# A two-layer decoder trunk on one core: weight halves formed by GpSimd transfers in the attention stages

## The chip, the cores and the metric

The kernel runs on one core of a Trainium2 chip. The time is device microseconds of one execution. A core has five engines that this text names: TensorE (PE, with its weight loads PEld), VectorE (DVE), ScalarE (ACT), GpSimd (POOL) and SyncE (SP). Each takes its own instructions strictly in order; they meet through semaphores. Transfers between HBM and the on-chip memory (SBUF) are issued by an engine's queue and carried out by 16 DMA engines.

## The reference

Two layers over 512 tokens of width 1024. Each has three parallel attention branches (differential, latent, and cross attention into 256 memory tokens), mixed by gates, and a squared-ReLU MLP of width 4096. All is float32.

```python
for l in range(DEPTH):
    h = rmsnorm(x, g_mix[l])
    dq, dk, dv, c_q, c_kv_kr, xq, gate_logits = jnp.split(h @ w_in[l], split_idx, axis=-1)
    y_diff = diff_attention(dq, dk, dv, ...) @ w_diff_o[l]
    y_mla = latent_attention(c_q, c_kv_kr, ...) @ w_mla_o[l]
    y_mem = memory_cross_attention(xq, rmsnorm(mem, mem_gain[l]), w_mem_kv[l], ...) @ w_cross_o[l]
    gates = jax.nn.sigmoid((gate_logits + b_gate[l]).reshape(B, S, N_BRANCHES, D))
    merged = gates[:, :, 0] * y_diff + gates[:, :, 1] * y_mla + gates[:, :, 2] * y_mem
    x = x + merged @ w_out[l]
    u = rmsnorm(x, g_mlp[l]) @ w_mlp1[l]
    x = x + jnp.square(jax.nn.relu(u)) @ w_mlp2[l]
```

## The kernel before, in words

**Three products for one.** Matmuls with weights run in the type float32r, which keeps fewer bits than float32. To keep the accuracy, each operand is split in two: a high half, which is the value rounded to float32r, and a low half, which is what the rounding lost. `mm3` (L108) multiplies high by high, high by low and low by high into one accumulator, at lines L109, L110 and L111.

**Weights come in units.** A unit is a tile of 128 x 1024 values (512 KB), the weights of one 128-wide output block or of half a 256-wide one; a few are smaller. There are 160 a layer. For each unit, `load_raw` issues a load from SyncE's queue into one of three tiles `wraw`; `do_split` calls `split_into`, in which ScalarE copies the tile into `whi` with rounding (L101) and VectorE subtracts, `wlo = wraw - whi` (L102). There are four buffers of `whi` and four of `wlo`. The loop at the end of the trunk keeps four units split ahead of the one that is used next, and three more loaded.

**The program is a list of entries.** An entry is a piece of a projection (with the units it uses) or a piece of attention (with none). In the attention stages `merge` interleaves the two kinds after the table `PLAN`, so that TensorE has projection matmuls while an attention step goes through softmax. Seven such stages follow each other in a layer: two of latent attention (beside the gates, then the memory's keys and values `w_mem`, the cross queries `w_xq` and the first differential projection `w_d`), one of cross attention and four of differential attention. Before them come the latent projections, after them the last gates, the output projections and the MLP, all without attention. A scheduler then places all instructions on their engines by its own estimate of times; the list gives it the dependencies and the buffers, and it may move instructions past each other.

**An attention step.** TensorE writes scores (`pss`, L610 and L613), VectorE adds the mask and finds the negative row maximum `nmx` (L622, L624), ScalarE takes the exponential into a tile `P` (L627; three buffers of 128 x 2 x 512), TensorE transposes `P` (L638, L654), ScalarE copies, TensorE multiplies by the values. A differential projection (`diff_chunk`, L553) is drained twice per chunk, once for each half of the tokens: ScalarE copies and squares (L564, L566), VectorE sums (L568), GpSimd takes an inverse square root `f` (L132), VectorE rotates meanwhile (L583 to L585) and multiplies by `f` (L587), TensorE transposes (L591). GpSimd does little else.

Of the kernel before, what the change touches and what calls it, by code (L numbers as in the profile page):

```python
# [9 lines left out]
F32 = mybir.dt.float32  # L10
F32R = mybir.dt.float32r
AF = mybir.ActivationFunctionType
ALU = mybir.AluOpType
AX = mybir.AxisListType

P = 128
# [22 lines left out]

class Entry:  # L40
    def __init__(self, fn, units=()):
        self.fn, self.units = fn, list(units)


def merge(att, gemm):
    if not att:
        return gemm
    out, n, m = [], len(att), len(gemm)
    j = 0
    for i, a in enumerate(att):  # L50
        out.append(a)
        while j < m and j * n < (i + 1) * m:
            out.append(gemm[j])
            j += 1
    out.extend(gemm[j:])
    return out
# [3 lines left out]
def tile_trunk(ctx: ExitStack, tc: tile.TileContext, x_t, mem_t, mem_n, pos, ifr, gcol, grow, w_ck, w_cq, w_kvb, w_qb,  # L60
               w_mem, w_xq, w_d, w_g, w_oc, w_om, w_od, w_out, w_1, w_2, out):
    nc = tc.nc
    V, A, G, T = nc.vector, nc.scalar, nc.gpsimd, nc.tensor

    def pool(name, bufs, **kw):
        return ctx.enter_context(tc.tile_pool(name=name, bufs=bufs, **kw))

    RB, NB = 3, 4
    cst = pool("cst", 1)
    sm = pool("sm", 2)  # L70
    pw_raw, pw_hi, pw_lo = pool("wraw", RB), pool("whi", NB), pool("wlo", NB)
    pools = {n: pool(n, b) for n, b in (("H", 16), ("O", 16), ("X", 8), ("G", 1), ("B", 24), ("scr", 5), ("PT", 4))}
    p_p = pool("P", 3)
    PS = {n: pool("ps_" + n, b, space=bass.MemoryType.PSUM) for n, b in (("acc", 2), ("s", 3), ("tp", 2), ("o", 1))}
# [3 lines left out]
    def nm(s):  # L78
        cnt[0] += 1
        return f"{s}{cnt[0]}"  # L80

    def tl(which, dt=F32):
        return pools[which].tile([P, 512], dt, tag=which, name=nm(which))
# [16 lines left out]
    def split_into(hi, lo, src):  # L100
        A.activation(out=hi, in_=src, func=AF.Copy)  # L101
        V.tensor_tensor(out=lo, in0=src, in1=hi, op=ALU.subtract)  # L102
# [116 lines left out]
    def feed(l, k, xt, gbase, dst, sqs):  # L219
        hi, lo = tl(dst, F32R), tl(dst, F32R)  # L220
        split_scaled(hi, lo, xt, gc[:, l, gbase + k:gbase + k + 1])
        if k == 0:
            A.activation(out=sqs, in_=xt, func=AF.Square)
        else:
            s = tl("scr")
            A.activation(out=s, in_=xt, func=AF.Square)
            V.tensor_tensor(out=sqs, in0=sqs, in1=s, op=ALU.add)
        return hi, lo

    def new_sqs():  # L230
        return tl("scr")
# [22 lines left out]
    prog = []  # L254
# [24 lines left out]
    def layer(l):  # L279
# [13 lines left out]
        def begin():  # L293
            if l == 0:
                sqs = new_sqs()
                h = []
                xts = []
                for k in range(KT):
                    xt = tl("X")
                    nc.sync.dma_start(out=xt, in_=x_t[k * P:(k + 1) * P, :])  # L300
                    xts.append(xt)
                    if k in (0, 2, 5):
                        load_raw()
                for k, xt in enumerate(xts):
                    h.append(feed(0, k, xt, C_MIX, "H", sqs))
                st["h"], st["sqs"] = h, sqs
            s["h"] = st["h"]
# [550 lines left out]
        def dpair(p):  # L858
            return diff_chunk(p, 0) + diff_chunk(p, 1) + diff_chunk(p, 2)

        e = [Entry(lambda w: begin())]
        gx = [gate_item(1, ft, "X") for ft in range(KT)]
        ym = [y4_item(w_om, "om", 1, fp, True) for fp in range(4)]
# [10 lines left out]
        def take(spec):  # L874
            r = []
            for t in spec.split():
                n, _, k = t.partition(":")
                k = int(k) if k else len(groups[n])
                r += groups[n][:k]
                groups[n] = groups[n][k:]  # L880
            return r
        phases = [[], mla_att(0) + mla_att(1), mla_att(2) + mla_att(3), cross, diff_att(0) + diff_att(1), diff_att(2) + diff_att(3),
                  diff_att(4) + diff_att(5), diff_att(6) + diff_att(7), []]
        for a, sp in zip(phases, PLAN):
            e += merge(a, take(sp))
        assert not any(groups.values())
        e += [y8_item(ft) for ft in range(KT)]
        e += [out_item(ft) for ft in range(KT)]
# [5 lines left out]
    for l in range(L):  # L894
        prog.extend(layer(l))

    units = [ap for e in prog for ap in e.units]
    raws, splits = [], []
    consumed = 0

    def load_raw():
        ap = units[len(raws)]
        a, b = ap.shape[1], ap.shape[2]
        t = pw_raw.tile([P, 1024], F32, tag="wraw", name=nm("wraw"))
        nc.sync.dma_start(out=t[:, :a * b].rearrange("p (a b) -> p a b", a=a), in_=ap)
        raws.append((t, a, b))

    def do_split():
        t, a, b = raws[len(splits)]
        hi = pw_hi.tile([P, 1024], F32R, tag="whi", name=nm("whi"))  # L910
        lo = pw_lo.tile([P, 1024], F32R, tag="wlo", name=nm("wlo"))
        split_into(hi[:, :a * b], lo[:, :a * b], t[:, :a * b])
        splits.append(tuple(z[:, :a * b].rearrange("p (a b) -> p a b", a=a) for z in (hi, lo)))

    for i, e in enumerate(prog):
        if i == 0:
            e.fn([])
            continue
        while len(splits) < min(len(units), consumed + NB):
            while len(raws) < min(len(units), len(splits) + RB):  # L920
                load_raw()
            do_split()
        while len(raws) < min(len(units), len(splits) + RB):
            load_raw()
        n = len(e.units)
        e.fn(splits[consumed:consumed + n])
        consumed += n


# [79 lines left out]
```

## Time and profile before

| | |
|---|---|
| median of 3 runs | 2035.33 us (2035.23 to 2035.63) |
| the profiled execution | 2039.67 us, of which the span of the profile is 2037.6 |
| layer 0: start and latent projections | 0 to about 130 us |
| layer 0: attention stages | about 130 to 600 us |
| layer 0: output projections and MLP | about 600 to 1020 us |
| layer 1: attention stages | about 1140 to 1607 us |
| bytes read from HBM | 175.06 MB, 88 GB/s over the span |

Busy time on TensorE is an engine's share with matmuls overlapping each other, so a TensorE that is always busy in a stretch did not wait in it. A row of waits names who waited, on which line, and who ended the wait. A granted clock under 1.00 means that TensorE ran slower for part of a stretch.

### The profile page before, as it was taken

Reading aid. Unit: us, or ns where it says so; the run is one execution under the profiler, and the core shown is the slowest. Engines: PE = TensorE matmul, PEld = TensorE weight load, DVE = VectorE, ACT = ScalarE, POOL = GpSimd, SP = SyncE. Lnnn points to the kernel's source line nnn. Section 1 sums busy time; section 2 is a strip of 40 time slices with the busy share of each in tenths; the row PEclk is TensorE's granted clock in tenths of the full one; section 3 lists DMA queues with packets and bytes.
Section 4 is the critical chain, followed back from the end, with each engine's and each line's share of the span. In section 5 each row is a group of like instructions: output and inputs, shape, how many; then the busy total and the mean of one; then the engine's idle time right before and its main releaser. Section 6 shows DMA issues by size and latency. Waiting matters only on the chain.

```text
span 2037.6 us, 27922 instructions
## 1 busy us (share of the span) xinstructions
PE 2005.1 (98%) x11008; PEld 1715.9 (84%) x11008; DVE 1162.2 (57%) x2170; ACT 917.4 (45%) x1727; POOL 146.0 (7%) x121
## 2 busy tenths in 40 slices
PE   8999999999999999999999999999999999999999
PEld 7779997888878888888888899979897788888887
DVE  7755765777656543434447567757686454434442
ACT  6666654444433432323346666634445334323321
POOL 0300110111200000000002001101020000000000
PEclk9989999999999999999999999999999999999999
DMA  5233122222214333333332321222222333333332
GB/s 170 73 110 102 69 63 73 63 73 73 63 53 154 93 96 101 93 99 98 117 104 67 125 80 63 72 74 63 73 63 63 101 116 93 102 96 94 102 94 73
DMA packets 54675, 181.06 MB, mean 89 GB/s; under 512 B 6416, under 2 KB 7440, under 8 KB 54544
## 3 DMA queue, kind: packets, MB, share of 16 engines
q1 hardware_dynamic: 51840, 175.66, 27.8%
q10 hardware_dynamic: 2704, 3.62, 0.6%
q8 instruction: 87, 1.43, 0.3%
q14 instruction: 44, 0.36, 0.1%
HBM read 175.06 MB, written 4.19 MB: 88 GB/s over the span
## 4 chain that ended last, share of the span: by engine, by line
PE 95%; ACT 2%; DVE 1%; DMA 1%; issue 0%; POOL 0%; ACTq 0%; DVEq 0%; POOLq 0%
PE psacc L109 21%; PE psacc L111 20%; PE psacc L110 20%; PE pss L109 7%; PE pss L111 7%; PE pss L110 7%; PE pss L610 2%; PE pss L613 2%; PE pso L642 2%; PE pstp L654 1%; PE pstp L638 1%; PE pstp L591 1%; PE pso L110 1%; PE pso L111 1%; PE pso L109 1%; PE pstp L479 1%
## 5 line engine op out<-in xcount | busy, mean ns | idle before, releaser
L101 ACT ACTIVATE whi<-wraw 128x1024 fp32r<-128x1024 f32 (+3 forms) x320 | 334.5, 1046 | 751.7 <-PE psacc L110 398.5
L102 DVE TENSOR_TENSOR wlo<-wraw,whi 128x1024 fp32r<-128x1024 f32 (+3 forms) x320 | 385.9, 1206 | 97.7 <-ACT whi L101 95.4
L109 PE MATMUL psacc<-H,whi 128*128 128x512 f32 x816 | 321.6, 394 | 2.6 <-ACT B L561 2.2
L110 PE MATMUL psacc<-H,whi 128*128 128x512 f32 x816 | 320.2, 392 | 0.0
L111 PE MATMUL psacc<-H,wlo 128*128 128x512 f32 x816 | 320.1, 392 | 0.0
L109 PE MATMUL psacc<-whi,H 128*128 128x256 f32 (+1 forms) x928 | 271.6, 294 | 10.3 <-ACT whi L101 6.8
L110 PE MATMUL psacc<-wlo,H 128*128 128x256 f32 (+1 forms) x928 | 265.1, 286 | 0.0
L111 PE MATMUL psacc<-whi,H 128*128 128x256 f32 (+1 forms) x928 | 264.3, 287 | 0.2 <-DVE H L106 0.2
L109 PE MATMUL pss<-O,whi 128*128 128x512 f32 x640 | 249.8, 392 | 1.6 <-ACT O L105 1.6
L110 PE MATMUL pss<-O,whi 128*128 128x512 f32 x640 | 250.8, 392 | 0.0
L111 PE MATMUL pss<-O,wlo 128*128 128x512 f32 x640 | 250.5, 392 | 0.0
L109 PEld LDWEIGHTS psacc<-whi,H 128*128 128x128 f32 x928 | 177.6, 192 | 17.8 <-ACT whi L101 6.8
L109 PEld LDWEIGHTS psacc<-H,whi 128*128 128x128 f32 x816 | 153.2, 188 | 36.0 <-ACT B L561 2.6
L111 PEld LDWEIGHTS psacc<-H,wlo 128*128 128x128 f32 x816 | 153.2, 188 | 33.6 <-issue 2.0
L110 PEld LDWEIGHTS psacc<-H,whi 128*128 128x128 f32 x816 | 153.3, 188 | 31.4 <-issue 0.7
L110 PEld LDWEIGHTS psacc<-wlo,H 128*128 128x128 f32 x928 | 178.2, 192 | 1.8 <-issue 1.0
L111 PEld LDWEIGHTS psacc<-whi,H 128*128 128x128 f32 x928 | 177.3, 192 | 1.0 <-DVE H L106 0.4
L840 DVE TENSOR_TENSOR X<-psacc,X 128x512 f32<-128x512 f32 x64 | 44.3, 692 | 207.1 <-PE psacc L111 207.1
L627 ACT ACTIVATE P<-pss,nmx 128x128 f32<-128x128 f32 (+2 forms) x224 | 115.1, 521 | 73.6 <-DVE nmx L624 47.5
L109 PEld LDWEIGHTS pss<-O,whi 128*128 128x128 f32 x640 | 120.4, 188 | 27.3 <-ACT O L105 2.0
L110 PEld LDWEIGHTS pss<-O,whi 128*128 128x128 f32 x640 | 121.1, 189 | 25.5 <-DVE O L106 0.3
L111 PEld LDWEIGHTS pss<-O,wlo 128*128 128x128 f32 x640 | 121.0, 189 | 24.9
(231 smaller groups left out, 3220.6 us busy)
## 6 DMA issues: line engine op xcount, KB each, us to landing
wraw<-in_w_dram SPq DMA_DIRECT2D x128, 512.0 KB, 3.6
wraw<-in_w_g_dram SPq DMA_DIRECT2D x48, 512.0 KB, 3.6
wraw<-in_w_d_dram SPq DMA_DIRECT2D x48, 512.0 KB, 3.6
wraw<-in_w_mem_dram SPq DMA_DIRECT2D x16, 512.0 KB, 3.7
wraw<-in_w_od_dram SPq DMA_DIRECT2D x16, 512.0 KB, 3.6
wraw<-in_w_out_dram SPq DMA_DIRECT2D x16, 512.0 KB, 3.7
X<-in_x_t_dram SPq DMA_DIRECT2D x16, 256.0 KB, 5.4
wraw<-in_w_xq_dram SPq DMA_DIRECT2D x8, 512.0 KB, 4.3
```

Source lines behind the costliest of these rows:

```text
L101: A.activation(out=hi, in_=src, func=AF.Copy)
L102: V.tensor_tensor(out=lo, in0=src, in1=hi, op=ALU.subtract)
L109: T.matmul(o, lhsT=l[0], rhs=r[0], start=first, stop=False, **kw)
L110: T.matmul(o, lhsT=l[0], rhs=r[1], start=False, stop=False, **kw)
L111: T.matmul(o, lhsT=l[1], rhs=r[0], start=False, stop=last, **kw)
L479: T.transpose(tp_[:96, t * P:(t + 1) * P], in_=src[t][:, h * 96:(h + 1) * 96], identity=ident)
L591: T.transpose(tp_[:, h * 256 + t * P:h * 256 + (t + 1) * P], in_=y[:, t * 256 + h * P:t * 256 + (h + 1) * P], identity=ident)
L610: T.matmul(sw[m][:, :max(N, 256)], lhsT=qk[m][0][a], rhs=qk[m][1][b], start=i == 0, stop=i == 2)
L613: T.matmul(sv[m], lhsT=qk[m][0], rhs=qk[m][1], start=True, stop=True)
L627: A.activation(out=pt[:, m, :N], in_=sv[m], func=AF.Exp, bias=nmx[:, m:m + 1], accum_out=ssum[m])
L642: T.matmul(o, lhsT=w[:, j * P:(j + 1) * P], rhs=vs(j), start=j == 0, stop=j == nb - 1)
L840: V.tensor_tensor(out=xt, in0=q, in1=xt, op=ALU.add)
```

## The change

In the attention stages a unit no longer passes through a raw tile. A transfer issued from GpSimd's queue reads the weights from HBM and casts them to float32r straight into `whi`. ScalarE writes the negated high half into `wlo`. A second transfer from GpSimd reads the same weights again and adds them onto `wlo`, which leaves weight minus high half. VectorE has no part in it. An entry is marked `dma` if it stands in a stage with attention: 61 units a layer.

Elsewhere a unit is loaded from SyncE's queue and split as before, except that its raw tile is one of the three buffers `P` of the attention weights; the pool `wraw` is gone. There are six buffers of `whi` (`NBH`) and four of `wlo` (`NBL`). `ahead` begins a load up to six units ahead, makes low halves up to four ahead and two loads behind (`LAG`), and issues the adding transfer one low half behind. The space for the descriptors of GpSimd's transfers is doubled.

```diff
@@ class Entry
-        self.fn, self.units = fn, list(units)
+        self.fn, self.units, self.dma = fn, list(units), False
@@ tile_trunk
-    RB, NB = 3, 4
+    NBH, NBL, LAG = 6, 4, 2
-    pw_raw, pw_hi, pw_lo = pool("wraw", RB), pool("whi", NB), pool("wlo", NB)
+    pw_hi, pw_lo = pool("whi", NBH), pool("wlo", NBL)
@@ layer
         for a, sp in zip(phases, PLAN):
-            e += merge(a, take(sp))
+            g = take(sp)
+            for x in g:
+                x.dma = bool(a)
+            e += merge(a, g)
@@ end of tile_trunk
+    def begin_load():
+        ap, dma = units[len(hi_t)]
         a, b = ap.shape[1], ap.shape[2]
+        if dma:
+            hi = halves(pw_hi, "whi", a, b)
+            G.dma_start(out=hi, in_=ap)
+            hi_t.append(hi)
+        else:
+            t = p_p.tile([P, 2, 512], F32, tag="P", name=nm("wraw")).rearrange("p a b -> p (a b)")[:, :a * b].rearrange("p (a b) -> p a b", a=a)
+            nc.sync.dma_start(out=t, in_=ap)
+            raw_t.append(len(hi_t))
+            hi_t.append(t)
+
+    def make_low():
+        n = len(lo_t)
+        ap, dma = units[n]
+        a, b = ap.shape[1], ap.shape[2]
+        if dma:
+            lo = halves(pw_lo, "wlo", a, b)
+            A.activation(out=lo, in_=hi_t[n], func=AF.Copy, scale=-1.0)
+        else:
+            t = hi_t[n]
+            hi_t[n], lo = halves(pw_hi, "whi", a, b), halves(pw_lo, "wlo", a, b)
+            split_into(hi_t[n], lo, t)
+            raw_t.remove(n)
+        lo_t.append(lo)
+
+    def add_low():
+        nonlocal added
+        ap, dma = units[added]
+        if dma:
+            G.dma_start(out=lo_t[added], in_=ap, accum_op=ALU.add)
+        added += 1
+
+    def ahead(need):
+        while True:
+            n = len(hi_t)
+            if n < len(units) and (n < consumed + NBH if units[n][1] else len(raw_t) < 3 and n < consumed + NBH + 2):
+                begin_load()
+                continue
+            m = len(lo_t)
+            if m < n and m < consumed + NBL and (m < need or m + LAG < n or not units[m][1]):
+                make_low()
+                continue
+            if added < m and (added < need or added + 1 < m):
+                add_low()
+                continue
+            return
@@ kernel
-    nc = _bacc.Bacc("TRN2", target_bir_lowering=False, num_devices=1, dynamic_dma_scratch_size=2048)
+    nc = _bacc.Bacc("TRN2", target_bir_lowering=False, num_devices=1, dynamic_dma_scratch_size=4096)
```

What moves on the engines is seen best at two places of layer 0. The first is GpSimd's queue where the first differential projections are drained. In the rows, `f` is the inverse square root that VectorE multiplies by, `e` and `ss` what it is taken of; the engines in square brackets are those it waits for. Before:

```order
L132 TENSOR_TENSOR f576_2569<-e575_2567,mhalf_120 128x8 [waits DVE_49,Pool_49]
L132 TENSOR_TENSOR f582_2618<-e581_2616,mhalf_120 128x8 [waits DVE_49,Pool_49]
L132 TENSOR_TENSOR f614_2776<-e613_2774,mhalf_120 128x8 [waits DVE_49,Pool_49]
L132 TENSOR_TENSOR f620_2825<-e619_2823,mhalf_120 128x8 [waits DVE_49,Pool_49]
L132 TENSOR_TENSOR f682_3170<-e681_3168,mhalf_120 128x8 [waits DVE_49,Pool_49]
```

At the same place in the changed kernel, where `DMASW` is a transfer from GpSimd's own queue:

```order
L912 DMA whi539_2487<-in_w_d_dram 128x1024 [waits DMASW2_49,PE_49]
L938 DMA wlo540_2489<-in_w_d_dram 128x1024 [waits DMASW3_49,Activation_49]
L132 TENSOR_TENSOR f554_2542<-e553_2540,mhalf_117 128x8 [waits DVE_49,Pool_49]
L912 DMA whi562_2608<-in_w_d_dram 128x1024 [waits DMASW4_49,PE_49]
L938 DMA wlo563_2610<-in_w_d_dram 128x1024 [waits DMASW5_49,Activation_49]
L132 TENSOR_TENSOR f560_2591<-e559_2589,mhalf_117 128x8 [waits DVE_49,Pool_49]
L912 DMA whi566_2663<-in_w_d_dram 128x1024 [waits DMASW6_49,PE_49]
L938 DMA wlo567_2665<-in_w_d_dram 128x1024 [waits DMASW7_49,Activation_49]
L132 TENSOR_TENSOR f590_2747<-e589_2745,mhalf_117 128x8 [waits DVE_49,Pool_49]
```

The inverse square roots followed each other; now a casting load, which waits for TensorE to leave a buffer, and an adding one, which waits for ScalarE, stand between the two `f` of a chunk.

The second place is ScalarE's queue in the memory projections (`w_mem`) of layer 0, where it empties accumulators (`scr<-psacc`, L342). Before:

```order
L101 ACTIVATE O318_1375<-pso367_1540 64x256 [waits DVE_49]
L342 ACTIVATE scr389_1660<-psacc380_1591 128x512 [waits PE_49]
L101 ACTIVATE whi396_1678<-wraw324_1413 128x1024
L344 ACTIVATE scr390_1662<-scr389_1660 128x512 [waits Activation_49]
L101 ACTIVATE whi400_1709<-wraw329_1447 128x1024 [waits DMAHW3_49,PE_49]
L342 ACTIVATE scr417_1782<-psacc399_1684 128x512 [waits PE_49]
L101 ACTIVATE whi424_1800<-wraw383_1620 128x1024 [waits DMAHW0_49]
```

In the changed kernel:

```order
L101 ACTIVATE O311_1363<-pso358_1526 64x256 [waits DVE_49]
L926 ACTIVATE wlo387_1665<-whi319_1430 128x1024 [waits DMASW5_49,DMASW0_49,PE_49]
L342 ACTIVATE scr379_1645<-psacc371_1577 128x512 [waits PE_49]
L926 ACTIVATE wlo390_1695<-whi372_1602 128x1024 [waits DMASW7_49,DMASW2_49,PE_49]
L344 ACTIVATE scr380_1647<-scr379_1645 128x512 [waits Activation_49]
L926 ACTIVATE wlo413_1785<-whi386_1663 128x1024 [waits DMASW4_49,DMASW1_49,PE_49]
L342 ACTIVATE scr405_1765<-psacc388_1668 128x512 [waits PE_49]
```

A rounding copy of a raw tile has become a negated copy of a high half; it waits for a transfer from GpSimd's queue in place of one from SyncE's, and for TensorE to leave a buffer of `wlo`.

More of the change, by code (lines that the diff above doesn't have):

```diff
@@ L302, in begin @@
                     if k in (0, 2, 5):
-                        load_raw()
+                        begin_load()
                 for k, xt in enumerate(xts):
@@ L895, in tile_trunk @@
         prog.extend(layer(l))
[L897 to L902, printed above, removed]
-        a, b = ap.shape[1], ap.shape[2]
[L904 to L913, printed above, removed]
+    units = [(ap, e.dma) for e in prog for ap in e.units]
@@ new lines, in tile_trunk, with halves @@
+    hi_t, raw_t, lo_t = [], [], []
+    added = consumed = 0
+    def halves(pw, tag, a, b):
+        return pw.tile([P, 1024], F32R, tag=tag, name=nm(tag))[:, :a * b].rearrange("p (a b) -> p a b", a=a)
+    def begin_load():
+        ap, dma = units[len(hi_t)]
+        a, b = ap.shape[1], ap.shape[2]
+        if dma:
[7 more added lines that the diff above has]
+            hi_t.append(t)
@@ new lines, in ahead @@
+    def ahead(need):
+        while True:
+            n = len(hi_t)
+            if n < len(units) and (n < consumed + NBH if units[n][1] else len(raw_t) < 3 and n < consumed + NBH + 2):
+                begin_load()
+                continue
[7 more added lines that the diff above has]
+            return
@@ L918, in tile_trunk @@
             continue
[L919 to L924, printed above, removed]
         n = len(e.units)
-        e.fn(splits[consumed:consumed + n])
+        ahead(consumed + n)
+        assert added >= consumed + n
+        e.fn([(hi_t[k], lo_t[k]) for k in range(consumed, consumed + n)])
         consumed += n
```

## The prediction

> **What bounds the kernel now.** I read the page first, then one table of stretches, then the waits of TensorE, then single instructions.
>
> ```profile
> span 2037.6 us, 27922 instructions
> ...
> PE 2005.1 (98%) x11008; PEld 1715.9 (84%) x11008; DVE 1162.2 (57%) x2170; ACT 917.4 (45%) x1727; POOL 146.0 (7%) x121
> ...
> PE 95%; ACT 2%; DVE 1%; DMA 1%; issue 0%; POOL 0%; ACTq 0%; DVEq 0%; POOLq 0%
> ```
>
> The second line gives busy time by engine, the third the chain of waits that ended last. TensorE (PE) is busy for 98% of the span and holds 95% of the chain. The change leaves every matmul in place, so it can win only what TensorE loses by waiting, and only in the attention stages. The table of stretches (columns: stretch in us, its length, busy us of PE, PEld, DVE, ACT and POOL, granted clock, share of the DMA engines, GB/s) shows the two attention parts, each cut at the end of the memory projections, with a piece of the MLP between them:
>
> ```profile
> 130.00:182.00 52.00, 47.43 (x310) 42.23 (x310) 34.82 (x70) 37.46 (x86) 2.71 (x3) 0.90 0.37 119
> 182.00:600.00 418.00, 415.02 (x2718) 365.88 (x2716) 274.80 (x602) 212.32 (x472) 50.74 (x36) 1.00 0.21 66
> 650.00:1000.00 350.00, 350.00 (x1553) 289.92 (x1552) 153.25 (x178) 114.52 (x146) 1.01 (x1) 1.00 0.32 97
> 1140.00:1192.00 52.00, 50.52 (x356) 45.87 (x355) 33.99 (x66) 38.46 (x86) 2.87 (x2) 0.97 0.32 104
> 1192.00:1607.00 415.00, 412.17 (x2680) 362.71 (x2678) 274.70 (x605) 210.51 (x468) 45.12 (x28) 1.00 0.22 67
> ```
>
> TensorE's idle time in the four attention stretches is 4.57 + 2.98 + 1.48 + 2.83 = 11.9 us. The clock takes 0.10 x 52 = 5.2 us and 0.03 x 52 = 1.6 us more. That is the **ceiling** of any gain, some 19 us or 0.9%, although VectorE (DVE) is busy two thirds of these stretches.
>
> How much of it is VectorE's? TensorE's waits (us in total, times, longest) over the whole span, and the four instructions behind one of them (start, length, engine, line, what; in brackets the idle time and who ended it):
>
> ```profile
> PE psacc L109 <- ACT scr L564: 2.2, 2, 1.1
> PE psacc L109 <- ACT B L561: 2.2, 2, 1.1
> ...
> PE pss L610 <- ACT P L627: 0.3, 2, 0.2
> ...
> 502.84 1.22 DVE L102 TENSOR_TENSOR wlo<-wraw,whi 128x1024 fp32r<-128x1024 f32 x1
> ...
> 505.26 0.58 ACT L627 ACTIVATE P<-pss,nmx 128x384 f32<-128x384 f32 x1 [1.07 <-DVE nmx L624]
> ...
> 507.41 0.60 ACT L564 ACTIVATE scr<-psacc 128x512 f32<-128x512 f32 x1
> ...
> 508.06 0.38 PE L109 MATMUL psacc<-whi,H 128*128 128x256 f32 x1 [1.11 <-ACT scr L564]
> ```
>
> VectorE forms a weight's low half for 1.22 us at 502.84; the row maximum behind it comes late, ScalarE (ACT) waits 1.07 us for that, empties the accumulator late, and TensorE stands for 1.11 us. This is the chain that the change cuts.
>
> **The change part by part.** Removed: VectorE's subtraction for each unit of weights in the attention stages.
>
> ```profile
> L102 DVE TENSOR_TENSOR wlo<-wraw,whi 128x1024 fp32r<-128x1024 f32 x61 | 74.4, 1220 | 20.5 <-ACT whi L101 19.2 <-PE psacc L111 1.1
> ...
> L101 ACT ACTIVATE whi<-wraw 128x1024 fp32r<-128x1024 f32 x61 | 64.5, 1058 | 81.8 <-PE psacc L110 55.0 <-PE psacc L111 26.8
> ...
> 1500.00:1550.00 50.00, 47.62 (x309) 41.55 (x308) 36.46 (x96) 25.92 (x64) 7.77 (x4) 0.97 0.20 63
> ```
>
> These are the groups of 130 to 600 us: 61 units a layer, 122 in all, 74.4 us of VectorE a layer. ScalarE keeps one pass of the same shape for each unit, 1058 ns, now a negated copy. What reaches the end is only the three waits quoted above, 2.2 + 2.2 + 0.3 = 4.7 us, and the clock that falls behind one of them, 0.03 x 50 = 1.5 us near 1513. **Gain: 6.2 us**, between 0 (if ScalarE is late for its other work too) and the ceiling, 19 + 1.5 us.
>
> Added: each unit is read from HBM twice, both times by a transfer issued on GpSimd. No accumulating or casting transfer is in this trace. The nearest rows:
>
> ```profile
> wraw<-in_w_mem_dram SPq DMA_DIRECT2D x16, 512.0 KB, 3.7
> ...
> 139.11 0.58 PE L109 MATMUL psacc<-whi,O 128*128 128x256 f32 x1 [2.58 <-ACT O L105]
> ...
> L109 PE MATMUL psacc<-whi,O 128*128 128x256 f32 x64 | 19.4, 306 | 2.6 <-ACT O L105 2.6
> ...
> 172.01 0.48 DVE L106 SCALAR_TENSOR_TENSOR B<-psacc,rmem,B 128x256 fp32r<-128x256 f32 x1 [0.78 <-ACT B L105]
> ```
>
> A plain 512 KB load lands 3.7 us after its issue. In the MLP stretch 97 GB/s take 0.32 of the 16 engines, so full rate is 303 GB/s and one load is 524,288 B / 303 GB/s = 1.73 us of all engines. The tight place is the memory projections: the first of their 64 matmuls of that line (8 a unit, so 8 units) starts at 139.1 and the last result is taken at 172.0, so a unit is used every 32.9 / 8 = 4.1 us. With both transfers at the plain price a unit needs 3.5 us and fits. An accumulating transfer must also read the tile that it adds to; I take it at two plain loads, 3.46 us, which makes 5.2 us a unit, 1.1 us over, 8.7 us over 8 units. The lead hides part: a low half is made up to four units ahead, which leaves three periods, 12.3 us, for a negated copy of 1.06, an issue of about 1 and a landing of some 4, so about 6 us are spare (12.3 - 6.1). Left over: 2.7 us a layer, and a clock drop of about 1.6 us as in the 0.97 rows. **Loss: 2 x 4.3 = 8.6 us**, between 0 (plain price) and, with cast and sum at twice and three times the plain price, 8.7 us a unit. That is more than the mean spacing of all attention units, 470 / 61 = 7.7 us, and 122 x 1.0 us would be lost.
>
> The Trainium skill, DMA: Bandwidth & Descriptors, section "Issuing engines are not separate DMA queues", says that transfers from ScalarE, SyncE and GpSimd run on the same 16 engines and interleave. By that rule GpSimd adds no bandwidth and the doubled bytes lie on the engines of the 0.32 row; if GpSimd's queue had engines of its own, the 8.6 us would be nothing. This trace, with no transfer from GpSimd in it, cannot tell. The same page's fit for GpSimd's transfers (section "Anatomy of one DMA — SWDGE (gpsimd) path"), 2.0 us plus bytes over 436 GB/s, gives an estimate of 3.2 us for one of these, near the row's 3.7.
>
> Moved: GpSimd's queue was nearly empty, and now two transfers a unit stand in it among the inverse square roots `f` that VectorE needs.
>
> ```profile
> L132 POOL TENSOR_TENSOR f<-e,mhalf 128x8 f32<-128x8 f32 x16 | 33.8, 2114 | 92.3 <-DVE e L573 54.9 <-DVE e L575 37.3
> ...
> L132 POOL TENSOR_TENSOR f<-e,mhalf 128x4 f32<-128x4 f32 x6 | 6.0, 1008 | 68.7 <-DVE e L383 44.7 <-DVE e L348 24.0
> ...
> L584 DVE TENSOR_TENSOR scr<-scr,ra 128x256 f32<-128x256 f32 x32 | 12.6, 414 | 0.0
> L583 DVE TENSOR_TENSOR scr<-scr,rb 128x256 f32<-128x256 f32 x32 | 12.2, 419 | 0.0
> ```
>
> An `f` takes 2.1 us and is covered by about as much rotary work (2 x 0.41 + 2 x 0.42 and one sum). The second `f` of a chunk now stands behind a load that waits for TensorE and an accumulating one that waits for ScalarE. An issue costs GpSimd between 0 and the 2.1 us of `f`; I take 1.0, the row of its small operation. So 8 such `f` a layer come about 2 us late. VectorE then stands 16 us a layer, but it has won 74. TensorE sees it only where the turned projection is next in its queue: I take 1 us a layer, **2 us**, between 0 and 32.
>
> Raw tiles move into the three buffers `P` of the attention weights. Behind the last attention units raw loads for the gates already hold two of them.
>
> ```profile
> L627 ACT ACTIVATE P<-pss,nmx 128x256 f32<-128x256 f32 x38 | 17.9, 479 | 14.2 <-DVE nmx L624 6.9 <-PE pstp L654 3.9 <-DVE nmx L618 3.3
> ```
>
> With three buffers ScalarE already waits 3.9 us for transposes (L654) to free one. For two or three units a layer with one or two buffers I take 1 us of TensorE a layer, **2 us**, between 0 and 3 x 3.9 a layer.
>
> **Sum.** -6.2 + 8.6 + 2 + 2 = +6.4 us. Against the profiled execution's own 2039.67 us (2037.6 of span and 2.1 around it) that is 2046.1; the median of the runs, 2035.33, lies 4.34 below, so I forecast **2042 us**, 0.3% slower.
>
> **The rivals.**
> - *VectorE's relief wins* (faster). If the accumulating transfer costs hardly more than a plain one, the memory projections keep up and 6.2 us stay: about 2029, or down to 2016 if all idle time and clock loss go. It decides at 4.1 us for both transfers of a unit. For it: the share of the engines is only 0.21 outside the memory projections. Against it: 0.37 there already, at half the bytes.
> - *Hidden anyway*: TensorE idles 3 us in 418, the relief pays for the late `f` and the shared buffers, and the time stays within 4 us of 2035.
> - *The transfers become the bound*: at over 7.7 us a unit, 2075 to 2160. Nothing in the rows excludes it, since none shows such a transfer.
> - *VectorE isn't relieved*: the low halves leave it, but it stands for `f` instead; at 16 us a layer against 74 this can only eat part of the gain, so it goes with "hidden".
>
> **How the numbers follow.** Forecast (supply falls behind in the memory projections, 2036 to 2060): 0.43, of which 0.05 within 0.2%. Relief wins: 0.28. Hidden: 0.17. Transfers bound: 0.12. What a measurement tells from no change is 0.2%, 4 us. So faster 0.28, same 0.22, slower 0.50. The range leaves out the lower end of the gain (0.08) and most of the transfer-bound case (0.11): 2022 to 2090.
>
> **What would show it.** Right: 130 to 182 and 1140 to 1192 longer, with a DMA share above 0.7 and TensorE waiting for a transfer into wlo; no wait near 508, 523, 1513 and 1530. Wrong on the price: the landing of wlo's transfers at 4 us or less, and no such wait. Wrong on GpSimd: VectorE's wait at L587 for `f` stays at zero. Transfers bound: a DMA share near 1 all through 182 to 600. The forecast falls if an accumulating transfer costs under 1.4 plain ones (then faster) or over 3 (then far slower).

## The result, and the profile after

The changed kernel takes 2054.29 us (median of 4 runs, 2053.48 to 2056.57), the kernel before on the same chip 2035.48: a ratio of 1.0092, 95% interval 1.0075 to 1.011. It is 18.8 us slower. That is the side that was forecast and inside the range, but three times the +6.4 us of the sum.

Three lines of the page of the changed kernel: span, busy time by engine, and the chain of waits.

```profile
span 2054.5 us, 27940 instructions
...
PE 2009.3 (98%) x11008; PEld 1717.5 (84%) x11008; DVE 1023.5 (50%) x2048; ACT 919.7 (45%) x1727; POOL 319.7 (16%) x365
...
PE 93%; issue 2%; DMA 2%; ACT 2%; DVE 1%; POOL 1%; ACTq 0%; POOLq 0%; DVEq 0%
```

VectorE lost 139 us of work, as meant. TensorE holds 93% of the chain in place of 95%, and transfers (DMA) now hold 2%. The stretches of the attention stages, with the columns of the prediction (busy us of PE, PEld, DVE, ACT and POOL, granted clock, DMA share, GB/s):

```profile
130.00:182.00 52.00, 42.69 (x274) 38.91 (x275) 21.21 (x51) 35.50 (x77) 14.21 (x19) 0.87 0.77 193
182.00:600.00 418.00, 416.38 (x2723) 365.61 (x2722) 230.63 (x565) 215.97 (x481) 112.12 (x124) 1.00 0.58 126
...
1140.00:1192.00 52.00, 47.94 (x308) 42.68 (x307) 20.05 (x45) 35.56 (x72) 16.29 (x22) 0.97 0.89 216
1192.00:1607.00 415.00, 413.38 (x2720) 363.61 (x2718) 230.08 (x566) 215.86 (x482) 107.74 (x117) 1.00 0.59 126
```

In the memory projections (first and third row) the DMA share went from 0.37 and 0.32 to 0.77 and 0.89, and TensorE idles 9.3 and 4.1 us where it idled 4.6 and 1.5. In the long stretches it idles 1.6 us each, less than the 3.0 and 2.8 of before: there the change helps. These stretches end at 600 and 1607 us, ahead of the last transposition of each layer's attention, which comes up below. TensorE's waits over the whole span (us in total, times, longest):

```profile
PE pstp L669 <- DVE scr L666: 8.5, 2, 4.2
...
PE pss L613 <- ACT P L627: 5.1, 1, 5.1
PE psacc L109 <- ACT O L105: 5.0, 2, 3.7
PE psacc L110 <- DMA wlo<-in_w_mem_dram: 4.5, 2, 2.8
...
PE psacc L109 <- ACT scr L564: 1.4, 2, 0.7
PE psacc L109 <- ACT B L561: 0.3, 2, 0.2
```

The last two are what is left of the waits that the change was to cut (2.2 each before). The first four are where it loses. The wait for `wlo` is the forecast one. The wait of 5.1 us for `P` is a cousin of it, in ScalarE's timeline (start, length, engine, line, what; in brackets idle time and who ended it):

```profile
125.17 0.35 ACTq L205 DMA_DIRECT2D B<-in_mem_n_dram  x1
125.70 0.19 ACT L206 ACTIVATION_READ_ACCUMULATOR B<-B 128x1 f32 x1
132.43 0.63 ACT L206 ACTIVATE B<-B 128x512 f32<-128x512 f32 x1 [6.54 <-DMA B<-in_mem_n_dram]
...
133.06 0.67 ACT L627 ACTIVATE P<-pss,nmx 128x512 f32<-128x512 f32 x1
```

ScalarE stands 6.54 us for a small load of the memory that shares the busy engines, and the softmax behind it comes late. In the kernel before, its longest such wait was 3.1 us:

```profile
128.53 0.63 ACT L206 ACTIVATE B<-B 128x512 f32<-128x512 f32 x1 [3.09 <-DMA B<-in_mem_n_dram]
```

The wait for L666 stands at the two ends of the attention, here in TensorE's timeline of layer 0:

```profile
604.44 0.39 PE L111 MATMUL pss<-O,wlo 128*128 128x512 f32 x1
604.66 1.05 PE L642 MATMUL pso<-B,PT 128*128 128x128 f32 x8
609.95 1.06 PE L669 MATMUL pstp<-ident,scr 128*128 128x128 f32 x4 [4.23 <-DVE scr L666]
```

The last head's product with the values (L642) is followed at once by its transposition (L669), and nothing lies between them while ScalarE, VectorE and GpSimd normalise. In the trace of before 14 matmuls of the output projection `w_od` (`pss<-O`) lie there, and the wait is 1.1 us; the first and the last line of that stretch:

```profile
595.26 1.05 PE L642 MATMUL pso<-B,PT 128*128 128x128 f32 x8
...
600.55 0.63 PE L669 MATMUL pstp<-ident,scr 128*128 128x128 f32 x4 [1.05 <-DVE scr L666]
```

From the end of L642 to the transposition it is 4.2 us in both kernels, so the 14 matmuls hide 3.2 us of the same work. Ahead of that transposition both programs have 63 of these matmuls in all; the scheduler put 49 of them ahead of the last L642 before, and all 63 in the changed kernel.

A table of all kernels puts the time by stretch. They are taken from one execution's trace, both layers added: **latent** from the first latent score (L613) to the first differential score (L610), with the memory projections in it; **differential** from there to the start of the last L669; **rest** is all else up to the start of the last matmul. The matmuls in a stretch are the same number in every kernel (1506 a layer in the latent, 1752 in the differential one), so a longer stretch is lost time and not more work. "Cover" is the number of matmuls between the last L642 and its L669 (in each layer; two numbers where the layers differ).

| kernel | ratio to before | latent | differential | rest | cover |
|---|---|---|---|---|---|
| before | 1 | 446.3 | 589.0 | 998.2 | 14 |
| changed | 1.0092 | 452.4 | 595.8 | 1002.2 | 0 |
| relief alone | 0.9917 | 435.5 | 583.0 | 995.9 | 17 |
| no second transfer | 1.0034 | 440.5 | 596.0 | 1001.7 | 0 |
| second transfer without addition | 1.0044 | 441.7 | 596.0 | 1003.7 | 0 |
| tail on the new path | 1.0024 | 449.9 | 582.4 | 1002.7 | 31 |
| the same, no second transfer | 0.9951 | 437.2 | 582.4 | 999.5 | 31 |
| the same, memory's loads on SyncE | 1.0007 | 448.1 | 582.4 | 1002.2 | 31 |
| and the addition at once | 1.0002 | 448.1 | 582.4 | 1003.1 | 31 |
| and the first load deeper, in place of it | 1.0008 | 448.7 | 582.5 | 1002.6 | 31 |
| own raw buffers, short lead | 1.0543 | 492.8 | 653.4 | 995.9 | 33, 25 |
| differential only, short lead | 1.0314 | 442.7 | 654.4 | 997.9 | 24, 25 |
| differential only, longer lead | 0.9943 | 439.3 | 582.4 | 997.3 | 32 |
| control: its order, old path | 0.9973 | 439.0 | 590.5 | 998.6 | 28 |

### The profile page after: what moved, and what is told of

Same layout as the page of the kernel before. It is cut to its first block, busy times and chain, and to the rows that moved or that the text cites. A ratio compares the mean times of both kernels' runs of the same rounds, so it can differ in the third digit from the quotient of the medians.

```text
span 2054.5 us, 27940 instructions
## 1 busy us (share of the span) xinstructions
PE 2009.3 (98%) x11008; PEld 1717.5 (84%) x11008; DVE 1023.5 (50%) x2048; ACT 919.7 (45%) x1727; POOL 319.7 (16%) x365
## 4 chain that ended last, share of the span: by engine, by line
PE 93%; issue 2%; DMA 2%; ACT 2%; DVE 1%; POOL 1%; ACTq 0%; POOLq 0%; DVEq 0%
PE psacc L109 20%; PE psacc L111 20%; PE psacc L110 20%; PE pss L109 7%; PE pss L110 7%; PE pss L111 7%; PE pss L610 3%; PE pss L613 2%; PE pso L642 2%; PE pstp L654 1%; PE pstp L638 1%; DMA wlo<-in_w_mem_dram 1%; PE pstp L591 1%; PE pstp L479 1%; PE pso L110 1%
## 5 line engine op out<-in xcount | busy, mean ns | idle before, releaser
L101 ACT ACTIVATE whi<-wraw 128x1024 fp32r<-128x1024 f32 (+3 forms) x198 | 206.1, 1041 | 599.2 <-DMA wraw<-in_w_dram 377.3
L102 DVE TENSOR_TENSOR wlo<-wraw,whi 128x1024 fp32r<-128x1024 f32 (+3 forms) x198 | 236.2, 1193 | 33.8 <-PE pss L111 13.5
L926 ACT ACTIVATE wlo<-whi 128x1024 fp32r<-128x1024 f32 x122 | 128.9, 1058 | 131.8 <-PE psacc L111 67.9
```

The costliest lines, as they stand in the source:

```text
L926: A.activation(out=lo, in_=hi_t[n], func=AF.Copy, scale=-1.0)
```

## The experiments

Theory 1: the second read and the addition keep the DMA engines busy in the memory projections. Theory 2: raw tiles in the three buffers `P` move the last head back, so that its tail is bare. The kernel before took 2036.3 to 2037.8 us on the chips of these runs; ratios are to it.

**Relief alone.** The kernel before, minus the subtraction.

```diff
-        split_into(hi[:, :a * b], lo[:, :a * b], t[:, :a * b])
+        if skip[len(splits)]:
+            A.activation(out=hi[:, :a * b], in_=t[:, :a * b], func=AF.Copy)
+            lo = hi
```

> The kernel before, with one thing taken out: in the attention stages VectorE's subtraction for the low half is left out (122 of 1220 ns each), and the high half is read in its place. This leaves the low halves of these weights out of the sums; matmuls, loads and everything else stay as they were. It prices the relief of VectorE alone. Relief as predicted: 2029 us (6.2 us less than the kernel before), with the waits of TensorE for L564 and L561 gone. Relief is worth nothing, because ScalarE is late for its other work too: 2034 to 2036 us. Relief is worth the whole ceiling: 2016 us.

Measured: 2020.03 us, ratio 0.9917 (0.9903 to 0.993). Leaving the subtractions out is worth 16.9 us, nearly as much as the whole ceiling. About half of it goes with the clock. The granted clock is 0.994 over 2037.6 us in the kernel before, some 12 us lost, and here:

```profile
core 0: 2018.5 us, clock 0.998
```

That is some 4 us lost. The waits of about 1 us near 508, 523, 601, 1148, 1513, 1530 and 1608 us became shorter or went, and with them all but one of six drops to half clock. The order of the work changed a little too (17 matmuls cover the tail in place of 14), and what an order alone can do is shown by the control, the last run.

**No second transfer.**

```diff
-        ap, dma = units[added]
-        if dma:
-            G.dma_start(out=lo_t[added], in_=ap, accum_op=ALU.add)
```

> The changed kernel without its second transfer: the low half stays the negated high half, so the weight itself is not added to it. ScalarE's copy, the casting first transfer and the shared P buffers stay. Theory 1 (the doubled bytes keep the DMA engines busy, which makes low halves and the small loads of the memory projections late): DMA share of 130 to 186 us near the 0.37 of before, TensorE's wait for wlo gone and the 5.1 us wait for P at 134 back near 2 to 3 us, so 4 to 6 us a layer less than the changed kernel: 2042 to 2046 us, while the waits of 4.2 us at the two ends of the attention stay. Theory 2 (the raw tiles in the three P buffers delay the end of the attention): these two waits of 4.2 us stay in full and the memory projections hardly change: 2052 to 2055 us. If transfers cause both: 2036 us or less.

Measured: 2043.83 us, 1.0034 (1.0021 to 1.0047), so the second transfer costs 0.0058 or 11.8 us. Nearly all goes from the latent stretch (452.4 to 440.5). TensorE's waits for `wlo` and for `P` go, though a wait of 7.5 us for `O` stands there in layer 0. The bare tail stays to the digit:

```profile
PE pstp L669 <- DVE scr L666: 8.5, 2, 4.2
```

Both theories hold, each for its place.

**Second transfer without the addition.**

```diff
-            G.dma_start(out=lo_t[added], in_=ap, accum_op=ALU.add)
+            G.dma_start(out=lo_t[added], in_=ap)
```

> The changed kernel with its second transfer a plain casting one: the weight overwrites the negated high half in place of being added to it, so the low half is left out of the result. The same bytes come from HBM over the same queue with the same waits; only the addition is gone. Theory 1 with the addition as the price (an adding transfer costs about two plain ones): landing into wlo falls from 8.4 to 5 to 6 us in the memory projections, TensorE's wait for wlo goes, about 4 us a layer less: 2045 to 2049 us. Theory 1 with the doubled bytes alone as the price: landing and time stay, 2053 to 2055 us. Theory 2: no change, 2053 to 2055 us.

Measured: 2045.95 us, 1.0044 (1.0031 to 1.0056): of the 11.8 us, 9.8 go with the addition and 2.0 with the doubled read, which the intervals can't tell from nothing. Queue 0 (GpSimd's) and the transfers of the memory's weights, of the changed kernel (packets, MB, share of 16 engines over the span; KB and median us to landing), and then of this one:

```profile
q0 software_dynamic: 35136, 127.94, 29.1%
...
whi<-in_w_mem_dram POOLq DMA_DIRECT2D x16, 512.0 KB, 5.6
wlo<-in_w_mem_dram POOLq DMA_DIRECT2D x16, 512.0 KB, 8.4
```

```profile
q0 software_dynamic: 35136, 127.94, 20.9%
...
wlo<-in_w_mem_dram POOLq DMA_DIRECT2D x16, 512.0 KB, 5.7
```

With the run before this one the three prices can be told apart. Its queue holds the first transfers alone:

```profile
q0 software_dynamic: 17568, 63.97, 10.9%
```

So 122 casting first transfers take 0.109 x 2042.3 = 223 us of all engines, 1.82 us each; 122 casting second ones 0.209 x 2045.5 - 223 = 205 us, 1.68 each; 122 adding ones 0.291 x 2054.5 - 223 = 375 us, 3.08 each. A cast costs what the plain load was worked out at (1.73); an addition costs 1.8 of them. A unit then needs 1.82 + 3.08 = 4.9 us of the engines where one is used every 4.1 us.

**Tail on the new path.** The last three gate units and the 8 units of `w_od` of each layer are loaded and split as in the attention stages, so no raw tile lies in `P` before the attention ends.

```diff
-        e += [y8_item(ft) for ft in range(KT)]
+        y8 = [y8_item(ft) for ft in range(KT)]
+        for x in g + y8:
+            x.dma = True
+        e += y8
```

> The changed kernel, whole computation, with the last units of the attention's last phase and the 8 w_od units behind it on the new path too, so that no raw tile shares the three P buffers before the attention has ended. Theory 2 (raw tiles in P delay the last head, whose tail then has nothing to cover it): the two waits of 4.2 us for L666 at the end of the attention fall to the 1.1 us of before, and with the clock that drops behind them 3 to 5 us a layer go: 2044 to 2049 us. If the late end comes from the transfers or from the order of the work instead: 2052 to 2056 us.

Measured: 2041.29 us, 1.0024 (1.0012 to 1.0035), 13.9 us less than the changed kernel. The differential stretch falls by 13.4 us, 31 matmuls cover the tail, and the wait is gone: the transposition starts as the last of them issues.

```profile
604.71 0.39 PE L111 MATMUL pss<-O,wlo 128*128 128x512 f32 x1
604.94 0.60 PE L669 MATMUL pstp<-ident,scr 128*128 128x128 f32 x4
```

This edit also takes 22 subtractions from VectorE; a run below keeps them and has the same 582.4 us.

**Own raw buffers.**

```diff
-    NBH, NBL, LAG = 6, 4, 2
+    NBH, NBL, LAG = 4, 4, 1
-    pw_hi, pw_lo = pool("whi", NBH), pool("wlo", NBL)
+    pw_raw, pw_hi, pw_lo = pool("wraw", 3), pool("whi", NBH), pool("wlo", NBL)
```

The memory for GpSimd's descriptors is 3072 in place of 4096, to make room, in this and the next runs with such buffers.

> The changed kernel, whole computation, with three raw buffers of their own (as before) in place of the sharing with P; the room comes from whi, 4 buffers in place of 6, so the new path runs one unit less deep. Theory 2 (a raw tile in one of the three P buffers makes the last head late): the two waits of 4.2 us for L666 go as in the run with the gates and w_od on the new path, and the time is within 4 us of that run's 2041 us, unless the shorter lead makes TensorE wait longer for wlo in the memory projections (then up to 2050 us). If it was not the sharing but the order in which the raw loads stand there: the waits of 4.2 us stay and the time is 2054 to 2060 us.

Measured: 2147.4 us, 1.0543 (1.0524 to 1.0562). No expectation came near. The bare tail is cured, but the differential stretch is 58 us longer and the latent one 40 us. The edit changed two things at once, the raw buffers and the depth and lead of the new path, and the second took over.

**Differential only.** The edit of the run above, and

```diff
-                x.dma = bool(a)
+                x.dma = bool(a) and j >= 4
```

> As the run with three raw buffers of its own, whole computation, with the new path only in the four differential phases; the units of the memory projections and of the latent and cross attention are loaded and split as before. Theory: the relief of VectorE (17.5 us in all, measured) lies partly in the differential phases, where the DMA engines have room (share 0.2 before), and the losses lie in the memory projections (additions and second loads) and in the shared P: 2022 to 2032 us, with no wait for wlo, no wait of 4.2 us for L666, and none near 508, 523, 1513 and 1530 us. Rival: GpSimd's issues delay its own inverse square roots f and so VectorE throughout the differential phases: 2036 to 2045 us. Rival: the relief lies in the early stages alone: 2033 to 2038 us.

Measured: 2100.36 us, 1.0314 (1.03 to 1.0329), again far off all three. Without a memory projection on the new path the loss is still there, so it isn't theirs. TensorE waits 28.6 us for `P`, and ScalarE's waits name the cause:

```profile
ACT wlo L926 <- DMA whi<-in_w_g_dram: 72.1, 22, 5.9
ACT wlo L926 <- DMA whi<-in_w_d_dram: 65.2, 18, 7.2
ACT wlo L926 <- DMA whi<-in_w_oc_dram: 46.4, 8, 7.2
```

ScalarE stands in order for a transfer that has only just been issued, because its issue stands in order on GpSimd behind the adding one, which waits for ScalarE's copy of the unit before:

```profile
353.53 0.86 POOL L938 DMA_DIRECT2D wlo<-in_w_g_dram  x1 [6.78 <-ACT wlo L926]
354.08 0.87 POOL L912 DMA_DIRECT2D whi<-in_w_oc_dram  x1
362.15 0.86 POOL L938 DMA_DIRECT2D wlo<-in_w_oc_dram  x1 [7.20 <-ACT wlo L926]
```

The first load goes out at 354 us, ScalarE copies at 360.80, the addition goes out at 362: two queues that wait for each other once a unit. In the changed kernel the same queue waits only for TensorE ahead of a first load, and under 1 us for ScalarE ahead of an addition (all six between 329 and 365 us).

**The tail on the new path, without the second transfer.** The edits of the second and the fourth run together.

> The run with the gates and w_od on the new path (2041 us), without its second transfer, so that the low half stays the negated high half (the weight is not added to it). If the two losses add, 12.5 us for the second transfer (from the changed kernel, 2054 to 2056, to the run without it, 2044) and 13 to 15 us for the shared P: 2028 to 2031 us, and the 8 to 11 us that are left above the run with the relief alone (2020) lie in the first, casting transfer on GpSimd. If they overlap (both make the same wait): 2034 to 2040 us. If they were the whole loss: 2018 to 2022 us.

Measured: 2025.9 us, 0.9951 (0.9938 to 0.9963), 2 us under what was expected if the losses add. The second transfer costs 14.9 us here, 12.7 of it in the latent stretch and **none** in the differential one: 582.4 us with it and without it, at a DMA share of about 0.65 in the run that has it.

**The memory's loads on SyncE.** The tail on the new path, and both small loads moved.

```diff
-                A.dma_start(out=mt, in_=mem_n[t * P:(t + 1) * P, j * 512:(j + 1) * 512])
+                nc.sync.dma_start(out=mt, in_=mem_n[t * P:(t + 1) * P, j * 512:(j + 1) * 512])
...
-                A.dma_start(out=raw.rearrange("p (k m) -> p k m", k=2), in_=mem_t[:, 2 * i:2 * i + 2, :])
+                nc.sync.dma_start(out=raw.rearrange("p (k m) -> p k m", k=2), in_=mem_t[:, 2 * i:2 * i + 2, :])
```

> The run with the gates and w_od on the new path (2041 us), whole computation, with the small loads of the memory (mem_n and mem_t) issued on SyncE instead of ScalarE. If ScalarE standing for these loads behind the doubled weights is what makes TensorE wait 4.7 us for P (L627) and 4.4 us for O (L105) around 134 and 146 us in that run: both waits fall under 2 us and the clock that drops behind them stays up, 2031 to 2036 us, with layer 1 unchanged. If these loads are late because the DMA engines are full, whichever queue issues them: 2039 to 2042 us.

Measured: 2038.34 us, 1.0007 (0.9999 to 1.0016), 3.5 us less (uncertain by some 3 us), just between the two expectations. The wait of 4.7 us for `P` is gone, that for `O` grew from 4.4 to 5.9 us: the loads of `mem_n` are no longer waited for, because SyncE issues them earlier (they land no faster, in up to 6.6 us), while those of `mem_t` are late wherever they are issued.

**Differential only, with a longer lead.** One line against the run of 2100 us:

```diff
-    NBH, NBL, LAG = 4, 4, 1
+    NBH, NBL, LAG = 5, 3, 2
```

> The run with the new path in the differential phases alone (2100 us), whole computation, with one thing changed: 5 buffers for whi and 3 for wlo in place of 4 and 4, and the negated copy two units behind the first load in place of one. Theory (lead): in that run ScalarE stands in its own queue, 5 to 7 us a unit, for a first load that it has only just let start, since the issue stands behind the adding transfer, which waits for ScalarE's copy of the unit before. With a unit more in between ScalarE no longer waits for whi in the differential phases, the 28.6 us of waits for P (L627) go, and the time falls to 2022 to 2034 us. Rival: GpSimd's queue itself, or the landing of 6 us, is the limit: 2080 us or more. Rival: the lead is cured, but the relief in these phases is worth nothing: 2034 to 2042 us.

Measured: 2025.23 us, 0.9943 (0.993 to 0.9955): 75 us gained by one buffer of `whi` more, one of `wlo` less, and a unit of lead between the load and the copy. The waits for `P` are gone, as the theory of the lead says; the three numbers were changed together. It is faster than both kernels, with the whole computation. Here the gates and `w_od` are loaded raw and split by VectorE, but into buffers of their own, and the differential stretch is at 582.4 us too. So the 13.4 us that the changed kernel lost there went with the sharing of `P`, not with the 22 subtractions: in every kernel whose raw tiles have buffers of their own 14 to 33 matmuls cover the tail, and in the three with raw tiles in `P` at that place none.

**The addition at once, and a deeper first load.** The run with the memory's loads on SyncE, with one line each changed:

```diff
-            if added < m and (added < need or added + 1 < m):
+            if added < m:
```

> The run with the memory's loads on SyncE (2038 us), whole computation, with the adding transfer put into GpSimd's queue right behind its negated copy, instead of one unit later. Theory: what is left of the second transfer's price is its lateness (TensorE waits 5.2 us for wlo in the memory projections, 3.1 us for w_od); half a unit to a unit earlier, most of these go: 2030 to 2036 us. Rival: the engines are full there and the landing only grows: 2037 to 2040 us. Rival: GpSimd now stands for ScalarE's copy, the first loads behind it come late, and so do the inverse square roots: 2042 us or more.

```diff
-    NBH, NBL, LAG = 6, 4, 2
+    NBH, NBL, LAG = 7, 4, 3
```

(and descriptor memory of 3072 in the second)

> The run with the memory's loads on SyncE (2038 us), whole computation, with the first load one unit earlier (7 buffers for whi and the copy three units behind; GpSimd's descriptor memory is 3072 in place of 4096 to make room). ScalarE's waits for whi in the memory projections (13.2 us in 3) should go. If these pass on to TensorE: 2030 to 2036 us. If the second transfer alone sets the pace there: 2037 to 2040 us. If the smaller descriptor memory holds up the issues: 2042 us or more.

Measured: 2037.85 us, 1.0002 (0.9993 to 1.0011), and 2039.73 us, 1.0008 (1.0 to 1.0017). Neither differs from the 1.0007 of their base. ScalarE's waits for `whi` in the memory projections went with the deeper first load, but TensorE's for `wlo` stay, at 4.5 and 4.3 us (5.2 in the base): more lead didn't help where the engines are short.

**The control.** The buffers and the loop of the run of 2025 us, with every unit on the old path (`j >= 9`, which no stage has).

> The control for the run with the new path in the differential phases and the longer lead (2025 us), whole computation: the same three raw, 5 whi and 3 wlo buffers and the same loop that sets the order, but no unit on the new path at all, so every weight is loaded once and split on ScalarE and VectorE as before. If the gain of that run is the new path's: 2034 to 2037 us, as the kernel before. If half of it is the new path's, and half comes from low halves that are made three units ahead in place of four (the memory projections, where it uses the old path too, took some 3 us a layer less in it than before): 2029 to 2032 us, with the differential phases at the 294 and 295 us of before (first scores to the last transposition) and not at 291. If all of it is the order and the buffers: 2023 to 2027 us.

Measured: 2032.17 us, 0.9973 (0.9963 to 0.9984), at the edge of the middle expectation, with differential phases of 295 us a layer. So 0.0027 of that run's gain, 5.5 us, is order and buffers, and 0.0030, about 6 us (uncertain by some 3), is the new path. In the traces the new path takes the differential stretch from 590.5 to 582.4 us and leaves the latent one, where it isn't used, as it is. Why the control's latent stretch is 7 us shorter than before (439.0 against 446.3) was not tried further: three low halves ahead in place of four, and another order, come together in it. It bears on the run with relief alone: that run's latent stretch is 10.8 us shorter, and here 7.3 us go with every subtraction in place.

## Why the prediction was right, and three times too small

By differences of ratios (each uncertain by some 3 to 4 us) the account is: relief -16.9 us; from there to the first transfer and its order +6.9 (0.9951 - 0.9917); second transfer +14.9; raw tiles in `P` +13.9; sum +18.8, which is the measured difference, as it must be along such a chain. The prediction had -6.2 + 8.6 + 2 + 2 = +6.4. The gain was 10.7 us larger than forecast and the losses together 23.1 us larger. The sign has luck in it: with the gain alone set right, the sum would have been -4.3 us, faster.

- **Gain, 6.2 us: measured 16.9 with the subtractions left out.** The mechanism was right in the differential stretch (VectorE late, then ScalarE, then TensorE): that run lost 6.0 us there, and the new path takes 8.1 off its control. The latent stretch lost 10.8 us and the rest 2.3. How much of the 10.8 is VectorE's relief is open, since the control loses 7.3 us there without any. Two things made the term small: only waits were counted whose releaser stood at L564, L561 or a differential `P`, and the clock was counted behind one of them. A wait of 1 us costs up to 2.7 by an estimate, since a half-clock interval of 3.4 us behind it costs TensorE up to 1.7. The ceiling of 19 us was a better guide than the sum, though its stretches end at 600 and 1607 us and so leave out the two tails, with their waits up to 600.6 and 1607.7 us and the half clock behind each.
- **Loss in the memory projections, 8.6 us: measured 14.9 for the second transfer, 12.7 of it in the latent stretch.** The price was nearly right (two plain loads taken, 1.8 measured; 5.2 us a unit taken, 4.9 measured), and so were the place, the wait for `wlo`, and a DMA share above 0.7. What the step left out is who else uses the engines: the memory's own small loads, which ScalarE waits for in order. The landing of 8.4 us in place of 4 took 4.4 of the "6 us" that were to spare.
- **Late `f`, 2 us: measured near nothing.** VectorE's waits at L587 are 3.1 us in the changed kernel and 1.3 before (its waits for any `f`, 21.0 and 14.7), and no differential stretch on the new path with a covered tail and enough lead is longer than the 583.0 us of relief alone. An issue costs GpSimd up to 0.87 us (the rows above), near the 1.0 taken, but its delay of `f` stays within what VectorE and TensorE have to spare. The 6.9 us between relief alone and the first transfer lie elsewhere, 3.6 of them in the rest; what makes them was not isolated. The table has a hint: every run with raw tiles in `P` has a rest of 999.5 us or more, every other one 998.6 or less.
- **Raw tiles in `P`, 2 us: measured 13.9.** This is the term that was mis-sized most. It was priced as a wait for a buffer, 1 us a layer. What the buffer did is to move work: the scheduler placed the last head behind all 63 matmuls that could have covered its tail. The prediction's rows show neither that tail nor what covers it. Each end then costs a wait of 4.2 us in place of 1.1 and 6.8 us of half clock in place of 3.4.
- **The rivals.** That relief wins was given 2016 to 2029 us, on the condition that the memory projections keep up; the run that leaves the second transfer out and cures the tail has 2025.9. Its stated condition, a second transfer at about the price of a plain one, was met without the cure in the run that only leaves out the addition: 2045.95, still slower, with the 13.9 us of the shared `P` in it. That the transfers become the bound for good was excluded by the share of 0.58 between the memory projections.
- **What would show it.** The stretches 130 to 182 and 1140 to 1192 us came out as forecast. The waits near 508 and 1513 us fell to 0.7 us each but didn't go.

The Trainium skill, DMA: Bandwidth & Descriptors, section "Issuing engines are not separate DMA queues", has transfers of all issuing engines on the same 16 engines. The runs agree: GpSimd's transfers raised the share of these engines to 0.89, and a small load from ScalarE's queue landed 7.2 us after its issue beside them, where it took 3.8 before.

## What to carry to other kernels

Price a transfer that adds at about two plain ones, and use it only where the DMA engines have room: here it was free in the differential stretch, at about one unit per 7.7 us, and cost 12.7 us in the latent one, with units down to one per 4.1. When two in-order queues feed each other (a load, a copy, an addition), count the units of lead between them first; a unit of lead, with the buffers it needs, was worth 75 us here, and one more than enough brought nothing. Before a buffer is shared, count the independent matmuls behind the last step of the stage that owned it, before and after: here the scheduler moved work when the buffer was shared, and the price was the bare tail, not the wait for the buffer.

## What the runs showed of the hardware

Half-clock intervals in all these traces, but for those that the end of the span cuts, last 3.4 us or a multiple (6.8, 10.2), and one can follow a gap of little over 1 us: in the kernel before TensorE stood 1.1 us up to 1513.7 us, and the clock was at one half for 3.4 us from 1513.8. Behind the gap of 4.23 us in the changed kernel it was at one half for 6.8 us:

```profile
604.00:609.90 5.90, 1.72 (x12) 1.41 (x10) 1.54 (x3) 1.23 (x2) 1.01 (x1) 1.00 0.00 0
610.00:616.80 6.80, 6.02 (x16) 4.56 (x17) 3.23 (x5) 1.76 (x3) 0.00 (x0) 0.50 0.01 2
616.80:625.00 8.20, 8.20 (x38) 6.75 (x37) 8.20 (x12) 4.09 (x6) 0.00 (x0) 1.00 0.77 226
```

In these two places the clock fell as the gap ended, and the work behind it paid. That isn't a rule: in the run without the second transfer it fell at 1610.6 us, 1.4 us before a like gap of 4.23 us ended. A gap doesn't always bring a drop either: the 1.11 us at 508 us in the kernel before brought none. And in the control the clock was at one half for 3.4 us from 521.8 us, behind no gap longer than 0.7 us (0.55, 0.68 and 0.23 us in the 3 us before). So the longest gap alone doesn't decide; what does was not tried. The Trainium skill, TensorE: Matmul & The Clock Gate, section "What's actually happening", gives a window of about 3.4 us, which these intervals agree with, and at least one idle window as what halves the clock; the drop behind a gap of 1.1 us differs from that, and by these traces a much shorter gap can be enough.
